# Twelve corner products of a split-fp32 encoder kernel as plain fp32 products of unsplit weights and tokens

## The chip, the cores and the metric

The kernel runs on one core of a Trainium2 chip. The metric is the time of one execution on the device in microseconds (us), lower is better. Engines are named as in the profile: PE is TensorE, DVE VectorE, ACT ScalarE, POOL GpSimd, SP SyncE, whose queue issues nearly all DMAs.

## The reference

A bidirectional encoder layer over 1280 tokens (1024 of a prompt, 256 of a sample), width 1024, all in fp32. What matters here is its beginning: a normalization, a modulation and one wide input projection.

```python
mod = c @ w_ada + b_ada
shift, scale, gate = jnp.split(mod[:, None, :], 3, axis=-1)
h = rms_norm(x, norm_g) * (1.0 + scale) + shift
p = h @ w_in                     # 1024 x 11280 weights
...
g_conv, g_mlstm = jnp.split(jax.nn.sigmoid(gmerge), 2, axis=-1)
merged = g_conv * (y_conv @ w_proj_conv) + g_mlstm * (y_m @ w_proj_mlstm)
return x + gate * (merged @ w_out)
```

The last 2048 columns of `w_in` (from `CGM` on) are the merge gates `gmerge`; the kernel multiplies with these first.

## The kernel before

**Split products.** PE multiplies fp32 operands in a form of one pass (`F32R`) that keeps only a part of the mantissa. To keep precision, each operand is split into a high part (a cast to `F32R`) and a low part (the operand less its high part), and a product is three passes: high x high, high weights x low tokens, low weights x high tokens (`go`, L737 to L760; the matmuls are all on L755). A weight block of 512 x 128 is split by `split_op`: the cast on ACT (L329), the difference on POOL (L330), into one of four `wh` and four `wl` buffers. Tokens are split by `both_parts`: ACT (L383), DVE (L384).

**Strassen.** The projection runs in the form of Strassen's algorithm on 2 x 2 blocks: the contraction of 1024 rows is cut into two halves of four tiles of 128 (k_ = 0 to 3), the tokens into halves of 640, and two column blocks of 128 form a pair. The transposed, modulated tokens are four quarters `B11, B21, B12, B22` of four tiles `xt` each (128 x 640). A pair needs seven products of one weight combination and one token combination each (`Strassen.jobs`), in the order 11 (tokens `b11`), 12 (`b21`), t2, t3, t1, t4, b22. A product is four pieces, one for each k_; a piece is 2 x 3 matmuls of 128 x 320. The weight combinations are made on DVE (`comb`, L628); c1, the first of them, needs both 512 KB halves (`raw`, j = 0 and 1) of the pair's weights. Results are added to earlier ones by DVE (`plus`, L672), which also frees the product's accumulator, one of three in PSUM.

**The corner products.** The products 11 and 12 of the first six pairs (columns 0 to 11 of the merge gates) need no combination. They run first, while the tokens are still being normalized: twelve products, on `b11` or `b21`, of the class `Corner` (L719). For each pair, `corner_load` (L338) fetches both weight blocks as one `raw` tile of 512 KB, and `corner_split` splits one block. There are three `raw` buffers.

**The beginning** (`beginning`, L393 on). SP loads w_ada and the tokens into tiles that later hold token parts; PE multiplies c with w_ada (L480, plain fp32); `norm_x` makes the row sums and scales the tokens (ACT L418, DVE L414 and the small operations L421 to L436); `turn_x` transposes 128 x 128 pieces on PE (L449), three and two at a time into one of two `misc` buffers of PSUM, from where ACT (L454) or DVE (L457) modulate them into `xt`. Groups of token chunks go in the order 0 to 2, 3 to 4, 5 to 7, 8 to 9. `combine` (L389) makes the sums and differences of quarters for t2, t3, t1 and t4, in place.

**What sets the order.** Every operation is recorded with an engine, an assumed duration and a step (`board.step`); `Board.order` then plays the record into one fixed order for each engine, by steps and assumed times. The engines wait for each other's semaphores and run their own lists strictly in order. SP's list is such a list too: a load that waits for its buffer holds up what stands behind it.

Of the kernel before, what the change touches and what calls it, by code (L numbers as in the profile page):

```python
# [9 lines left out]
F32 = mybir.dt.float32  # L10
F32R = mybir.dt.float32r
AF = mybir.ActivationFunctionType
ALU = mybir.AluOpType
# [3 lines left out]
P = 128  # L17
D = 1024
KT = D // P
# [11 lines left out]
TQ = T // 4  # L31
# [150 lines left out]
def encoder_kernel(  # L182
# [134 lines left out]
    def load(kb, dst, src, r, w, low=False):  # L317
        op("SP", kb, lambda: dma(dst(), src), r=r, w=w, low=low)
# [4 lines left out]
    def raw_tile():  # L323
        return buf(wp, [P, 4, 2 * P], F32, "raw", 3)
# [8 lines left out]
    raw_a, early = {}, {}  # L333

    def corner_split(n, j):
        raw = raw_a[n]
        return split_op(lambda: raw[:].rearrange("p a (b c) -> p (a b) c", b=2)[:, 4 * j:4 * j + 4, :], [raw])

    def corner_load(n):

        raw_a[n] = raw = raw_tile()
        load(512, lambda: raw[:].rearrange("p a (b c) -> p (a b) c", b=2), win[:, :, CGM + n * P:CGM + (n + 1) * P], (), [raw])
# [49 lines left out]
    def beginning():  # L392
# [67 lines left out]


# [7 lines left out]
        corner_load(0)  # L469
# [4 lines left out]
        corner_load(2)  # L474
# [10 lines left out]
        corner_load(4)  # L485
# [30 lines left out]
        early.update({(n, j): corner_split(n, j) for j in range(2) for n in (0, 2)})  # L516
        for kt in lows:
            board.step = kt - 6
            for cs in GROUPS[:2]:
                turn_x(cs, [kt])  # L520
            both_parts("b11", B11, [kt])
        for kt in lows:
            board.step = kt // 2 - 2
            for cs in GROUPS[:2]:
                turn_x(cs, [kt + 4])
            both_parts("b21", B21, [kt])
        for k in range(12):
            if k in (0, 2, 4):
                corner_load(6 + k)
            if k == 2:  # L530
                board.step = 0
                for cs in GROUPS[2:]:
                    norm_x(cs)
                for kt in lows:
                    board.step = 0 + kt // 2
                    for cs in GROUPS[2:]:
                        turn_x(cs, [kt, kt + 4])

                board.step = 3
                both_parts("b22", B22)  # L540
                combine(B22, B22, B12)
                board.step = 10
                combine(B12, B12, B11)
                board.step = 4
                combine(B11, B22, B11, ALU.add)
                both_parts("t2", B11)
                board.step = 5
                both_parts("t3", B22)
                board.step = 12
                combine(B21, B21, B11)  # L550
                singles("t1")
                both_parts("t1", B12)
                singles("t4")
                both_parts("t4", B21)
            go(k)
# [163 lines left out]
    class Corner:  # L719


        def __init__(self, n, st):
            self.n, self.st = n, st
            self.jobs = [(None, "b11", self.first), (None, "b21", st.e_12)]

        def first(self, acc):
            self.st.e_11(acc)

        def prep(self, j):
            return early.get((self.n, j)) or corner_split(self.n, j)  # L730

# [5 lines left out]
    def prep(k):  # L737
        if k < len(todo) and k not in made:
            board.step = k - (6 if k < 16 else 2)
            made[k] = todo[k][0].prep(todo[k][1])  # L740
# [466 lines left out]
    corners = {n: Corner(n, sts[n]) for n in sts}  # L1207
    for n, j in ((0, 0), (2, 0), (0, 1), (2, 1), (4, 0), (4, 1), (6, 0), (6, 1), (8, 0), (8, 1), (10, 0), (10, 1)):
        add(corners[n], [j])
# [636 lines left out]
```

## Time and profile before

| | us |
|---|---|
| median of 3 runs | 1730.31 |
| lowest, highest of them | 1727.86, 1730.43 |
| the profiled execution | 1726.71 |
| its span in the trace | 1724.6 |
| PE busy | 1676.9 (97%) |
| DVE, POOL, ACT busy | 974.6, 679.5, 604.4 |
| mean granted clock of PE | 0.992 |

Times within the trace are from the start of the span. PE's matmuls overlap: the duration of one holds its run-out, so what a row of them costs is read from start to start. "x2" is a row of two such instructions, and its duration goes from the first start to the last end. A bracket at the end of a row is the idle time before it and what ended it.

### The profile page before, as it was taken

The page shows a single profiled execution, that of the slowest core. Times are in us where ns is not written, and L with a number is a line of the kernel's source. Part 1 is how long each engine was busy: PE and PEld are TensorE (multiplying, and loading weights), DVE is VectorE, ACT ScalarE, POOL GpSimd, SP SyncE. Part 2 cuts the span into 40 slices and gives each one's busy share as a digit, 9 for nine tenths or more (in the row PEclk, how much of TensorE's full clock was granted, in tenths as well). Part 3 has the DMA queues.
Part 4 walks back from the last instruction along what each step waited for, and adds up shares of the span by engine and source line. Part 5 has one row for each costly group of instructions (what it writes and reads, how often), then busy time and mean ns, then how long its engine had stood idle before and what let it go on. Part 6 is the DMA issues. An engine that isn't in the chain of part 4 may idle for free.

```text
span 1724.6 us, 27940 instructions
## 1 busy us (share of the span) xinstructions
PE 1676.9 (97%) x10702; PEld 1591.3 (92%) x10702; DVE 974.6 (57%) x1657; ACT 604.4 (35%) x1185; POOL 679.5 (39%) x499
## 2 busy tenths in 40 slices
PE   7889999999999999999999999999999999999997
PEld 1789999899999999999999899999888889998986
DVE  1795433456555565566666765642247777565645
ACT  2753333224554222222222222222256565333322
POOL 1124333235665566667766533333210101323412
PEclk9899999999999999999999999999999999999999
DMA  9234323224553222222222434336878865684631
GB/s 332 87 109 146 115 91 121 64 74 122 148 155 108 57 68 68 80 80 63 65 61 89 141 108 138 117 117 231 284 232 273 269 199 162 219 282 135 229 112 61
DMA packets 217562, 241.88 MB, mean 140 GB/s; under 512 B 12645, under 2 KB 174677, under 8 KB 217429
## 3 DMA queue, kind: packets, MB, share of 16 engines
q1 hardware_dynamic: 217248, 240.06, 43.5%
q8 instruction: 85, 1.39, 0.3%
q14 instruction: 49, 0.39, 0.1%
q10 hardware_dynamic: 180, 0.04, 0.0%
HBM read 171.16 MB, written 68.89 MB: 139 GB/s over the span
## 4 chain that ended last, share of the span: by engine, by line
PE 91%; DVE 5%; issue 2%; ACT 1%; DMA 1%; ACTq 0%; SPq 0%; POOL 0%; DVEq 0%; POOLq 0%
PE acc L755 59%; PE u L1365 3%; PE qc L1347 3%; PE accd L1520 2%; PE accd L1521 2%; PE accd L1522 2%; PE accd L1733 2%; PE accd L1734 2%; PE accd L1732 2%; PE acc L1587 2%; PE acc L1588 2%; PE acc L1589 2%; PE acc L480 2%; PE misc L885 1%; PE misc L1408 1%
## 5 line engine op out<-in xcount | busy, mean ns | idle before, releaser
L672 DVE TENSOR_TENSOR q<-acc,q 128x640 f32<-128x640 f32 x272 | 220.6, 820 | 259.9 <-PE acc L755 249.5
L330 POOL TENSOR_TENSOR wl<-comb,wh 128x512 fp32r<-128x512 f32 x176 | 247.2, 1405 | 304.2 <-ACT wh L329 293.2
L330 POOL TENSOR_TENSOR wl<-raw,wh 128x512 fp32r<-128x512 f32 x136 | 191.6, 1409 | 250.9 <-ACT wh L329 245.1
L755 PE MATMUL acc<-xt,wh 128*128 128x320 f32 x1408 | 264.4, 310 | 0.0
L755 PEld LDWEIGHTS acc<-xt,wh 128*128 128x128 f32 x1408 | 220.6, 188 | 0.1
L329 ACT CAST wh<-comb 128x512 fp32r<-128x512 f32 x176 | 108.9, 619 | 243.6 <-PE acc L755 236.1
L329 ACT CAST wh<-raw 128x512 fp32r<-128x512 f32 x136 | 84.4, 621 | 286.5 <-PE acc L755 203.3
L755 PE MATMUL acc<-xt,wl 128*128 128x320 f32 x704 | 160.4, 309 | 0.0
L1548 POOL TENSOR_TENSOR wl<-raw,wh 128x512 fp32r<-128x512 f32 x28 | 36.3, 1300 | 233.7 <-ACT wh L1547 233.7
L755 PEld LDWEIGHTS acc<-xt,wl 128*128 128x128 f32 x704 | 117.7, 188 | 0.0
L628 DVE TENSOR_TENSOR comb<-raw 128x512 f32<-128x512 f32 x88 | 76.7, 872 | 46.7 <-DMA raw<-in_w_in_dram 31.2
L822 POOL TENSOR_TENSOR big<-big,q 128x640 f32<-128x640 f32 x48 | 78.8, 1641 | 37.1 <-DVE q L672 28.8
L572 ACT ACTIVATE q<-q,zero 128x640 f32<-128x640 f32 x76 | 63.2, 831 | 80.4 <-DVE q L672 74.8
L628 DVE TENSOR_TENSOR comb<-raw,comb 128x512 f32<-128x512 f32 x44 | 44.2, 1004 | 78.5 <-POOL wl L330 78.5
L755 PE MATMUL acc<-b00H,wh 128*128 128x320 f32 x352 | 83.0, 316 | 0.0
L755 PE MATMUL acc<-t2L,wh 128*128 128x320 f32 x352 | 80.3, 310 | 2.1 <-DVE t2L L384 2.1
L755 PE MATMUL acc<-b11H,wh 128*128 128x320 f32 x352 | 80.9, 310 | 1.5 <-ACT wh L329 1.5
L755 PE MATMUL acc<-t3H,wh 128*128 128x320 f32 x352 | 81.6, 313 | 0.0
L1520 PE MATMUL accd<-y,wh 128*128 128x320 f32 x256 | 79.9, 313 | 1.5 <-DVE og L1498 1.5
L755 PE MATMUL acc<-t2H,wh 128*128 128x320 f32 x352 | 80.8, 311 | 0.4 <-ACT t2H L383 0.4
L755 PE MATMUL acc<-b10H,wh 128*128 128x320 f32 x352 | 80.6, 309 | 0.4 <-DVE q L672 0.4
L755 PE MATMUL acc<-b11H,wl 128*128 128x320 f32 x352 | 80.1, 308 | 0.9 <-POOL wl L330 0.9
(320 smaller groups left out, 4195.4 us busy)
## 6 DMA issues: line engine op xcount, KB each, us to landing
raw<-in_w_in_dram SPq DMA_DIRECT2D x96, 256.0 KB
raw<-in_w_in_dram SPq DMA_DIRECT2D x46, 512.0 KB
th<-th_dr SPq DMA_DIRECT2D x32, 320.0 KB
th_dr<-q SPq DMA_DIRECT2D x28, 320.0 KB
raw<-in_w_proj_conv_dram SPq DMA_DIRECT2D x16, 512.0 KB
k<-kn_dr SPq DMA_DIRECT2D x64, 128.0 KB
raw<-in_w_proj_mlstm_dram SPq DMA_DIRECT2D x16, 512.0 KB
raw<-in_w_out_dram SPq DMA_DIRECT2D x16, 512.0 KB
```

Source lines behind the costliest of these rows:

```text
L329: op("ACT", .63, lambda: A.copy(wh[:], src()), r=r, w=[wh])
L330: op("POOL", 1.4, lambda: G.tensor_tensor(out=wl[:], in0=src(), in1=fp(wh[:]), op=ALU.subtract), r=[*r, wh], w=[wl])
L480: op("PE", .88, lambda h=h, j=j, kt=kt, wa=wa: PE.matmul(pada[h][0:4, j, :], cz4()[:, kt, :], wa()[:, j * 512:(j + 1) * 512], start=kt == ...
L572: A.activation(out, in_, AF.Tanh, bias=zero[:, 0:1], scale=0.5)
L628: op("DVE", .9, lambda: V.tensor_tensor(out=t[:], in0=x(), in1=y(), op=o), r=[x.tok, y.tok], w=[t])
L672: op("DVE", .82, lambda: V.tensor_tensor(out=two(dst()), in0=acc[:, :, 0:TQ], in1=two(t()), op=ALU.add), r=[acc, t.tok], w=[dst.tok])
L755: PE.matmul(acc[:, q, 0:TQ], st_[:, k_, :], m_[:, q * TQ:(q + 1) * TQ], start=k_ == 0 and n == 0, stop=k_ == 3 and n == 2)
L822: op("POOL", 1.65, lambda: G.tensor_tensor(out=dst(), in0=dst(), in1=t(), op=ALU.mult), r=[dst.tok, t.tok], w=[dst.tok])
L1347: PE.matmul(pq[:, 0:HD + 2], qTs[i][:, kd, c * P:(c + 1) * P], C[:, kd, :], start=kd == 0, stop=kd == 1)
L1365: PE.matmul(pu[:, db, 0:HD + 2], k[:, db * P:(db + 1) * P], wv[:], start=True, stop=True)
L1520: PE.matmul(accs[q][:, :TQ], wh, yH, start=kt == 0, stop=False)
L1548: op("POOL", 1.36, lambda wh=wh, wl=wl, src=src: G.tensor_tensor(out=wl[:], in0=src(), in1=fp(wh[:]), op=ALU.subtract), r=[raw, wh], w=[wl])
```

## The change

The twelve corner products become plain fp32 products: PE reads the unsplit weights in `raw` and the unsplit tokens in `xt`, two matmuls of 128 x 320 for each k_ instead of six. With that `Corner`, `corner_split` and their twelve splits on ACT and POOL go. The order of the twelve changes from pair by pair to first all six on `B11`, then all six on `B21`. A `raw` tile now holds one half (j) of the columns of two pairs, fetched by two DMAs of 256 KB. `b11` and `b21`, the split parts of the first two quarters, are still made, for the later pairs, but recorded beside the combinations. The steps of the preparations of the next products (`prep`) move from k - 6 to k - 8, up to k = 20.

```diff
-    def corner_split(n, j):
-        raw = raw_a[n]
-        return split_op(lambda: raw[:].rearrange("p a (b c) -> p (a b) c", b=2)[:, 4 * j:4 * j + 4, :], [raw])
-
-    def corner_load(n):
-
-        raw_a[n] = raw = raw_tile()
-        load(512, lambda: raw[:].rearrange("p a (b c) -> p (a b) c", b=2), win[:, :, CGM + n * P:CGM + (n + 1) * P], (), [raw])
+    def early_load(j, n):
+
+        raw_a[j, n] = raw_a[j, n + 2] = raw = raw_tile()
+        for i in range(2):
+            c = CGM + (n + 2 * i) * P
+            load(256, lambda i=i: raw[:, :, i * P:(i + 1) * P], win[:, 4 * j:4 * j + 4, c:c + P], (), [(raw, i)])
...
+        def early_product(k, j, x):
+
+            n = 2 * (k % 6)
+            raw, i = raw_a[j, n], n // 2 % 2
+            board.step = k
+            acc = buf(psX, [P, 2, 512], F32, "acc", 3)
+
+            def mm(k_):
+                for q in range(2):
+                    PE.matmul(acc[:, q, 0:TQ], raw[:, k_, i * P:(i + 1) * P], x[k_][:, q * TQ:(q + 1) * TQ],
+                              start=k_ == 0, stop=k_ == 3)
+
+            for k_ in range(4):
+                op("PE", 1.1, lambda k_=k_: mm(k_), r=[(raw, i), (x[k_], 0), (x[k_], 1)] + ([acc] if k_ else []), w=[acc])
+            (sts[n].e_12 if j else sts[n].e_11)(acc)
...
-        early.update({(n, j): corner_split(n, j) for j in range(2) for n in (0, 2)})
-        for kt in lows:
-            board.step = kt - 6
+        for kt in range(KT):
+            board.step = kt - 6 if kt < 4 else kt // 2 - 4
             for cs in GROUPS[:2]:
                 turn_x(cs, [kt])
-            both_parts("b11", B11, [kt])
+        for k in range(6):
+            early_product(k, 0, B11)
...
+        board.step = 1
+        both_parts("b22", B22)
+        combine(B22, B22, B12)
+        board.step = 8
+        both_parts("b11", B11)
+        combine(B12, B12, B11)
+        board.step = 3
+        combine(B11, B22, B11, ALU.add)
+        both_parts("t2", B11)
+        board.step = 4
+        both_parts("t3", B22)
+        for n in (0, 4, 8):
+            board.step = 2 + n // 2
+            early_load(1, n)
+        for k in range(6, 12):
+            early_product(k, 1, B21)
+        board.step = 10
+        both_parts("b21", B21)
+        combine(B21, B21, B11)
...
-            board.step = k - (6 if k < 16 else 2)
+            board.step = k - (8 if k < 20 else 2)
...
-    corners = {n: Corner(n, sts[n]) for n in sts}
-    for n, j in ((0, 0), (2, 0), (0, 1), (2, 1), (4, 0), (4, 1), (6, 0), (6, 1), (8, 0), (8, 1), (10, 0), (10, 1)):
-        add(corners[n], [j])
+    todo.extend([None] * 12)
```

PE's list at the first corner product, before (L449 are transposes; `b00H`, `b00L` are the parts of `B11`):

```order
L449 MATMUL misc<-ident,t3H 128x128 x2
L449 MATMUL misc<-ident,t3L 128x128 x2
L449 MATMUL misc<-ident,b11H 128x128
L449 MATMUL misc<-ident,t3H 128x128 x2
L449 MATMUL misc<-ident,t3L 128x128 x2
L449 MATMUL misc<-ident,b11H 128x128
L449 MATMUL misc<-ident,t3H 128x128 x2
L449 MATMUL misc<-ident,t3L 128x128 x2
L449 MATMUL misc<-ident,b11H 128x128
L755 MATMUL acc<-b00H,wh 128x320 x2
L755 MATMUL acc<-b00L,wh 128x320 x2
L755 MATMUL acc<-b00H,wl 128x320 x2
```

and after (L447 are the transposes, L468 the plain products):

```order
L447 MATMUL misc<-ident,t3H 128x128 x2
L447 MATMUL misc<-ident,t3L 128x128 x2
L447 MATMUL misc<-ident,b11H 128x128
L447 MATMUL misc<-ident,t3H 128x128 x2
L447 MATMUL misc<-ident,t3L 128x128 x2
L447 MATMUL misc<-ident,b11H 128x128
L468 MATMUL acc<-xt,raw 128x320 x2
L447 MATMUL misc<-ident,t3H 128x128 x2
L447 MATMUL misc<-ident,t3L 128x128 x2
L447 MATMUL misc<-ident,b11H 128x128
L468 MATMUL acc<-xt,raw 128x320 x2
```

The first piece of a product stands behind ten transposes instead of fifteen, and one piece follows each group of transposes; 34 pieces follow the last.

DVE's list where the corner products end, before: the last low parts (t1, t4), the sums, then the combinations for the first pair's last product and the second pair.

```order
L384 TENSOR_TENSOR xt_1062<-xt_152,xt_1024 128x640
L384 TENSOR_TENSOR xt_1071<-xt_153,xt_1035 128x640
L384 TENSOR_TENSOR xt_1079<-xt_154,xt_1045 128x640
L672 TENSOR_TENSOR q_1087<-acc_980,big_468 128x640
L672 TENSOR_TENSOR q_1095<-acc_1026,q_1087 128x640
L672 TENSOR_TENSOR big_468<-acc_1026,big_468 128x640
L628 TENSOR_TENSOR comb_1099<-raw_745,comb_814 128x512
L672 TENSOR_TENSOR q_1087<-acc_1064,q_1087 128x640
L628 TENSOR_TENSOR comb_1107<-raw_823,raw_857 128x512
L628 TENSOR_TENSOR comb_1112<-comb_1107,raw_823 128x512
```

and after (`q_771` is the sum of the last corner product, `raw_716` and `raw_736` are the second pair's weights, L382 the low parts of t4, `big_396<-acc_729` the sum of t2):

```order
L683 TENSOR_TENSOR q_771<-acc_697,q_594 128x640
L639 TENSOR_TENSOR comb_784<-raw_716,raw_736 128x512
L639 TENSOR_TENSOR comb_803<-comb_784,raw_716 128x512
L382 TENSOR_TENSOR xt_812<-xt_151,xt_748 128x640
L639 TENSOR_TENSOR comb_821<-raw_716 128x512
L382 TENSOR_TENSOR xt_831<-xt_152,xt_758 128x640
L382 TENSOR_TENSOR xt_843<-xt_153,xt_769 128x640
L382 TENSOR_TENSOR xt_851<-xt_154,xt_786 128x640
L683 TENSOR_TENSOR big_396<-acc_729,big_396 128x640
```

The second pair's combinations now stand ahead of the low parts of t4 and of the sum of t2.

POOL's list from its first split on, after (before, twelve splits of `raw` tiles of the corner products stand ahead of those of the combinations; `comb_695`, `comb_700`, `comb_704`, `comb_710` are the first pair's combinations, `raw_643` and `raw_685` its weights, and the second pair's `raw_736` goes into the buffer of `raw_685`):

```order
L330 TENSOR_TENSOR wl_712<-comb_700,wh_706 128x512
L330 TENSOR_TENSOR wl_726<-comb_704,wh_714 128x512
L330 TENSOR_TENSOR wl_746<-comb_695,wh_720 128x512
L330 TENSOR_TENSOR wl_761<-raw_685,wh_724 128x512
L330 TENSOR_TENSOR wl_794<-comb_710,wh_780 128x512
```

The split that reads `raw_685` is the fourth in the row.

## Rows read from the trace of the kernel before

**Rows 1.** The page, part 4: shares of the chain that ended last, by engine.

```profile
PE 91%; DVE 5%; issue 2%; ACT 1%; DMA 1%; ACTq 0%; SPq 0%; POOL 0%; DVEq 0%; POOLq 0%
```

**Rows 2.** Table by stretches: length; busy us of PE, PEld, DVE, ACT, POOL; clock; DMA.

```profile
140.00:160.00 20.00, 20.00 (x139) 20.00 (x138) 10.35 (x13) 6.23 (x9) 6.67 (x7) 1.00 0.37 113
```

**Rows 3.** Timeline of PE, 43 to 70 us: start, duration, line, operation, count, wait.

```profile
43.55 0.33 PE L449 MATMUL misc<-ident,t3H 128*128 128x128 f32 x1 [3.60 <-DVE t3H L436]
...
50.60 0.69 PE L449 MATMUL misc<-ident,t3H 128*128 128x128 f32 x2
...
51.70 0.88 PE L755 MATMUL acc<-b00H,wh 128*128 128x320 f32 x2
...
54.85 0.46 PE L755 MATMUL acc<-b00H,wl 128*128 128x320 f32 x2
...
69.29 0.27 PE L449 MATMUL misc<-ident,t2L 128*128 128x128 f32 x1
...
69.39 0.27 PE L449 MATMUL misc<-ident,t2H 128*128 128x128 f32 x1
```

**Rows 4.** Timeline of PE, 84 to 88 us: first matmuls of two products.

```profile
84.11 0.45 PE L755 MATMUL acc<-b00H,wh 128*128 128x320 f32 x2
...
87.62 0.45 PE L755 MATMUL acc<-b10H,wh 128*128 128x320 f32 x2
```

**Rows 5.** Timeline of PE, 105 to 133 us: products t2 to b22 of the first pair.

```profile
106.01 0.46 PE L755 MATMUL acc<-t2H,wh 128*128 128x320 f32 x2
...
110.97 0.56 PE L755 MATMUL acc<-t2L,wh 128*128 128x320 f32 x2 [2.10 <-DVE t2L L384]
...
113.09 0.73 PE L755 MATMUL acc<-t2L,wh 128*128 128x320 f32 x2
...
117.59 0.75 PE L755 MATMUL acc<-xt,wh 128*128 128x320 f32 x4
...
126.28 0.57 PE L755 MATMUL acc<-b11H,wh 128*128 128x320 f32 x2 [1.49 <-ACT wh L329]
...
131.05 0.47 PE L755 MATMUL acc<-t2H,wh 128*128 128x320 f32 x2
```

**Rows 6.** Timeline of PE: plain fp32 matmuls of L1347 and L480.

```profile
1296.04 1.03 PE L1347 MATMUL qc<-C,qT 128*128 128x258 f32 x4
...
1296.91 1.03 PE L1365 MATMUL u<-wv,k 128*128 128x258 f32 x4
...
14.68 3.60 PE L480 MATMUL acc<-b00L,big 128*4 128x512 f32 x8
...
18.11 3.60 PE L480 MATMUL acc<-b10H,big 128*4 128x512 f32 x8
```

**Rows 7.** Timeline of POOL and DVE, 38 to 43 us.

```profile
38.37 3.73 POOL L330 TENSOR_TENSOR wl<-raw,wh 128x512 fp32r<-128x512 f32 x3 [14.09 <-ACT wh L329]
...
40.21 0.67 DVE L504 SCALAR_TENSOR_TENSOR s<-big,cols 128x16 f32<-128x16 f32 x1
...
41.08 1.03 DVE L428 TENSOR_TENSOR rt<-rr 128x3 f32<-128x3 f32 x1
...
42.15 0.16 DVE L429 TENSOR_TENSOR rt<-rt,ssq 128x3 f32<-128x3 f32 x1
```

**Rows 8.** Timelines of SP's queue and DVE: a load and its first reader.

```profile
129.14 0.39 SPq L318 DMA_DIRECT2D raw<-in_w_in_dram  x1
...
133.12 0.81 DVE L628 TENSOR_TENSOR comb<-raw 128x512 f32<-128x512 f32 x1 [1.04 <-DMA raw<-in_w_in_dram]
```

**Rows 9.** Timelines of POOL and DVE, 112 to 134 us.

```profile
129.29 4.09 POOL L330 TENSOR_TENSOR wl<-comb,wh 128x512 fp32r<-128x512 f32 x3 [1.33 <-ACT wh L329]
...
115.24 3.02 DVE L384 TENSOR_TENSOR xt<-xt 128x640 fp32r<-128x640 f32 x4
...
126.93 1.57 DVE L628 TENSOR_TENSOR comb<-comb,raw 128x512 f32<-128x512 f32 x1
...
131.25 0.82 DVE L672 TENSOR_TENSOR big<-acc,big 128x640 f32<-128x640 f32 x1 [1.54 <-PE acc L755]
```

More of the change, by code (lines that the diff above doesn't have):

```diff
@@ L331, in split_op @@
         return wh, wl
-    raw_a, early = {}, {}
-    def corner_split(n, j):
-        raw = raw_a[n]
-        return split_op(lambda: raw[:].rearrange("p a (b c) -> p (a b) c", b=2)[:, 4 * j:4 * j + 4, :], [raw])
-    def corner_load(n):
-        raw_a[n] = raw = raw_tile()
-        load(512, lambda: raw[:].rearrange("p a (b c) -> p (a b) c", b=2), win[:, :, CGM + n * P:CGM + (n + 1) * P], (), [raw])
+    raw_a = {}
+    def early_load(j, n):
[3 more added lines that the diff above has]
+            load(256, lambda i=i: raw[:, :, i * P:(i + 1) * P], win[:, 4 * j:4 * j + 4, c:c + P], (), [(raw, i)])
     xt = {jl: [buf(xp, [P, TH2], F32, "xt", 17, xp.tile([P, TH2], F32, tag="xt", name="xt")) for _ in range(4)]
@@ L468, in beginning @@
             load_wa(kt)
-        corner_load(0)
+        early_load(0, 0)
         for kt in range(5, KT):
@@ L473, in beginning @@
             load_x(c)
-        corner_load(2)
+        early_load(0, 4)
         pada = [buf(psX, [P, 2, 512], F32, "acc", 3) for _ in range(2)]
@@ L484, in beginning @@
             load_x(c)
-        corner_load(4)
+        early_load(0, 8)
         mods = {}
@@ L515, in beginning @@
             norm_x(cs)
-        early.update({(n, j): corner_split(n, j) for j in range(2) for n in (0, 2)})
-        for kt in lows:
-            board.step = kt - 6
+        for kt in range(KT):
+            board.step = kt - 6 if kt < 4 else kt // 2 - 4
             for cs in GROUPS[:2]:
                 turn_x(cs, [kt])
-            both_parts("b11", B11, [kt])
-        for kt in lows:
[L523 to L555, printed above, removed]
+        for k in range(6):
+            early_product(k, 0, B11)
@@ new lines, in beginning @@
+        board.step = -1
+        for cs in GROUPS[2:]:
+            norm_x(cs)
+        for kt in lows:
+            board.step = -1 + kt // 2
+            for cs in GROUPS[2:]:
+                turn_x(cs, [kt, kt + 4])
+        board.step = 1
[8 more added lines that the diff above has]
+        board.step = 4
@@ L556, in beginning @@
+        both_parts("t3", B22)
[7 more added lines that the diff above has]
+        combine(B21, B21, B11)
+        singles("t1")
+        both_parts("t1", B12)
+        singles("t4")
+        both_parts("t4", B21)
         at[0] = 12
@@ L717, in corner_place @@
         return corner_places[i]
[L719 to L730, printed above, removed]
     todo, made, at = [], {}, [0]
```

## The prediction, made before the change was run

> **What bounds the kernel now.** The page's chain of waits comes first: TensorE (PE) makes 91% of the chain that ends last [rows 1], so a change is worth what it takes from or adds to PE's line, and other engines count where PE waits for them. The table by stretches comes second: from 140 us on PE is busy for all of 20 us at full clock [rows 2]. PE's order is the same in both programs from the first pair of gate columns on, and that of the other engines from the third pair on, so what the change does must show by one mark: the start of the second pair's first product, at 131.05 us in the trace of before [rows 5]. The rest is a shift.
>
> The timeline of PE up to that mark comes third. The first transpose of the tokens stands at 43.55 [rows 3]. From there to 131.05 are 87.5 us. What PE has to do in them at full clock: a split product takes 3.51 us (84.11 to 87.62) [rows 4], so twelve corner products are 42.1 and five of the first pair 17.6; 80 transposes at 0.107 (69.29 to 69.39) [rows 3] are 8.6. That is 68.3, so 19.2 us are lost. I place them so. The first product stands at 51.70, behind fifteen transposes, while DVE normalizes: 6.5 lost. The clock then is at the lower level, 1.2 GHz, until about 54.5, some 2.8 us behind the first product (by 54.85 two matmuls take 0.46 instead of 0.73 us) [rows 3, 5]: 1.4. Products t2 and t3 should take 7.0 but last from 106.01 to 117.59: 4.55 lost, 2.10 of them a wait for the low part of t2 from DVE and about 1.8 a second spell at 1.2 GHz behind it (0.73 us for two matmuls) [rows 5]. The first pair's last product waits for its weights (1.49 and more at 126.28): 117.59 to 131.05 is 13.46 for 10.5, 2.9 lost [rows 5]. The remaining 3.8 are short waits between transposes at 65 to 95 us.
>
> **The change, part by part.**
>
> 1. PE's work. A split product issues 24 matmuls of 320 columns at 0.1463 us each. A plain fp32 one issues 8, and each is two instructions in the trace: L1347 has two for each 258 columns, and four start to start take 0.87 us (1296.04 to 1296.91), 0.2175 each; L480 has eight of 512 columns in 3.43 us (14.68 to 18.11), 0.429 each [rows 6]. Scaled to 320 columns these two bounds give 0.270 and 0.268; I take 0.269. So one product is 16 x 0.269 = 4.31 us, twelve 51.7: **9.6 us more work**. The weight loads stay hidden: L1347 loads 128 x 128 fp32 at the 0.2175 pace, shorter than 0.269. The Trainium skill (FP8 and Floating Point Precision, TensorE Precision Notes) says a true fp32 product takes four passes; taken as four against three passes of the split form, that would make 56.2 and 14.1 more. The rows decide against that ratio, as a 320-column pass of the split form already costs 0.146 where a quarter of the plain one costs 0.1345.
>
> 2. The start. POOL's early weight splits go: its first split is now one of the first pair. In before three of them run from 38.37 for 3.73 us, and in that stretch tiny DVE operations take 0.67 and 1.03 us instead of 0.16 [rows 7]. These stand on the way to the first transpose. The Trainium skill (SBUF — State Buffer, SBUF: two separate sides) says that DVE and GpSimd share a pair of ports under a lock held for a whole instruction; the 1.03 agrees with it. Of the excess 0.51 + 0.87 I take **1.2 us**. The order of PE's instructions further puts the first product behind ten transposes instead of fifteen, without a cast before it: the eleventh starts at 50.60 [rows 3], and a product in its place would stand at about 50.7. So the first product moves from 51.70 to 50.7 - 1.2 = **49.5**, with 70 transposes left instead of 65.
>
> 3. The corner on PE. If nothing waits, product 10 of 12 ends at 49.5 + 1.4 (the same spell at low clock) + 70 x 0.107 + 40 x 1.077 = **101.5**, and product 12 at 110.1. The short waits between transposes I cost at nothing: each group of transposes now has a 1.08 us piece of plain product, ready since its weights need no split, in front of the next, and evacuating it takes DVE and ACT no longer than that. If this cover fails, up to 3.8 us return. The parts b00 and b10 are now made behind the transposes; when the transposes are through, at 49.5 + 1.4 + 7.5 + 14 pieces x 1.077 = 73.5, DVE has some 28 operations of 0.755 to make (3.02 for four) [rows 9], 21 us, and so the parts of t2 and t3 are ready before PE asks for them at 110. The 4.55 go. The weight combinations of all products of the first pair now stand in one row on DVE, ahead of the low parts of t4, so the 2.9 for the last product go too.
>
> 4. The new wait. Raw weight tiles are now read by PE itself, so each of the three buffers is held until its two products end, where before ACT and POOL emptied it ahead of them. The second half of the first pair (raw_685) can be fetched only when product 10 ends, 101.5. A 512 KB load lands about 3.9 us after its issue (129.14 to 133.12, where DVE waits for it) [rows 8]. Then: two combinations on DVE 1.4, cast 0.7, and on POOL four splits in a row of 1.36 (4.09 for three) [rows 9] = 5.45, of which the fourth reads raw_685. Only then SP can load raw_736 into that buffer: 3.9. DVE meanwhile stands at comb_784, which needs raw_736, with everything behind it: combinations 2.05, four low parts of t4 3.0, and the sum that frees the accumulator of t2, 0.82 [rows 9]. Product t4 needs both the low part and that accumulator. Sum 101.5 + 3.9 + 1.4 + 0.7 + 5.45 + 3.9 + 5.9 = 122.75. Where POOL and DVE meet, a combination took 1.57 where another took 0.81 [rows 8, 9]; I add 0.4: **123.1**. PE asks for t4 at 110.1 + 3 x 3.51 = 120.6, so it **waits 2.5 us**. Bounds: with no collision and loads of 3.4 us 1.1; with two collisions and loads of 4.4 4.5.
>
> 5. The clock behind that wait. In before a wait of 2.10 with shorter ones around it was followed by a spell at 1.2 GHz (1.8 us), the one of 1.49 with another just behind it was not [rows 5]. I take half, 0.9; ends 0 and 1.8.
>
> Sum: t4 123.1 + 2 x 3.51 + 0.9 = **131.0** at the mark, against 131.05: **no change**. The profiled execution took 1726.7 us for its span of 1724.6, which is 3.6 under the median of the runs shown, 1730.3; a change of 0.0 on that median is 1730.3. A measurement can tell about 0.2%, 3.5 us, from no change.
>
> **The rivals.**
>
> A, the gain stays. The loads land in 3.4 us, nothing collides, and the clock rises as early against the denser start as the better of the two cases allows: 1.4 less from the wait, 0.9 from the clock behind it, up to 1.4 from the first spell, at most 3.7 in all: 1726.6. For it: t2 and b22 waits worth 7.4 us go for certain. Against it: the chain of part 4 hangs on product 10, so an earlier PE only waits longer unless the loads are short. Chance 0.17 for more than 3.5 us.
>
> B, slower by the wait for t4. Its place is DVE at comb_784, its price whatever DVE ends behind 120.6. At 4.5 us of wait and a following spell of 1.8 the mark is 133.9, and with the lost cover of one more microsecond among the transposes 134.9: 1734.2. It decides from the point where raw_736 lands later than about 119, 2.2 us later than in my sum, or POOL's splits take 1.7 instead of 1.36 in a row. For it: 1.57 for one combination [rows 9]. Against: POOL has nothing else then. Chance 0.14.
>
> C, plain products cost more than their two passes say. On the Trainium skill's four against three passes (part 1) they would cost 4.5 us more than in my sum. As a mechanism of this kernel: at 0.293 per instruction, twice the split form's 0.146, forty pieces before product 10 end 3.8 us later, and all behind them: 134.8, 1734.1. Against it stands that L1347 runs at 0.2175 for 258 columns [rows 6]. Chance 0.06.
>
> **How the numbers follow.** Forecast, within 0.2%: 0.63; A 0.17; B and C 0.20. The forecast alone spans 1727.0 to 1733.6. The range of 1726.5 to 1734.5 takes in A and the nearer part of B and C, and leaves out some 2 in 10.
>
> **What would show it.** The 192 plain instructions some 0.27 us apart; the first one at 49 to 50 us; no DVE operation of a few columns over 0.3 us before 43; product t2 without a wait at 110; a PE wait of 1 to 4.5 us ahead of t4, named by DVE, with DVE idle for about 5 us before a combination that waits for a DMA; the second pair at 129 to 134. I am wrong if PE waits among the transposes again, if t2 waits, or if t4 doesn't.

## The result, and the profile after

The changed kernel takes 1733.19 us (median of 8 runs, 1731.75 to 1733.95), the kernel before, on the same chip, 1727.93 (8 runs, 1725.92 to 1730.43). The ratio is 1.0028, 95% interval 1.0017 to 1.0039: slower by about 5 us. The forecast was no change, 1730.3. Its range of 1726.5 to 1734.5 holds the time, but the slowdown is clear of the noise and none was forecast.

| | before | after |
|---|---|---|
| profiled execution, its span (us) | 1726.71, 1724.6 | 1732.88, 1731.1 |
| PE busy | 1676.9 | 1684.3 |
| POOL, ACT busy | 679.5, 604.4 | 662.7, 598.7 |
| first transpose, first corner product | 43.55, 51.70 | 41.94, 48.88 |
| product t2 of the first pair | 106.01 | 109.13 |
| second pair's first product, the mark | 131.05 | 136.68 |

The mark is 5.6 us later, the span 6.5, so nearly all of it happened ahead of the mark. PE's share of the chain that ended last has fallen from 91% [rows 1]. Page of the changed kernel, part 4:

```profile
PE 88%; DVE 3%; issue 1%; ACT 1%; DMA 0%; SPq 0%; DVEq 0%; ACTq 0%
```

The table by stretches of the changed kernel (columns as in [rows 2]) shows where:

```profile
80.00:100.00 20.00, 20.00 (x76) 14.13 (x75) 16.67 (x22) 10.61 (x15) 0.00 (x0) 1.00 0.40 134
100.00:120.00 20.00, 20.00 (x108) 17.07 (x106) 12.59 (x13) 8.09 (x12) 8.76 (x5) 1.00 0.44 135
120.00:140.00 20.00, 13.05 (x72) 12.99 (x72) 15.47 (x17) 4.98 (x7) 6.05 (x4) 0.74 0.36 117
140.00:160.00 20.00, 20.00 (x139) 20.00 (x138) 9.24 (x11) 6.23 (x9) 7.79 (x6) 1.00 0.44 135
```

From 80 us on PE has no gap up to 120 us, and then loses 6.95 of 20 us and a quarter of its clock. The timeline of PE, changed kernel, names the place (L447 transposes, L468 plain products, L753 split products):

```profile
41.94 0.33 PE L447 MATMUL misc<-ident,t3H 128*128 128x128 f32 x1 [2.23 <-DVE t3H L434]
...
48.88 2.16 PE L468 MATMUL acc<-xt,raw 128*128 128x320 f32 x4
...
51.42 1.24 PE L468 MATMUL acc<-xt,raw 128*128 128x320 f32 x4
...
72.76 36.77 PE L468 MATMUL acc<-xt,raw 128*128 128x320 f32 x136
...
109.13 0.69 PE L753 MATMUL acc<-t2H,wh 128*128 128x320 f32 x2
...
127.04 1.41 PE L753 MATMUL acc<-xt,wh 128*128 128x320 f32 x4 [6.95 <-DVE big L683]
...
128.77 1.27 PE L753 MATMUL acc<-xt,wh 128*128 128x320 f32 x4
...
130.37 1.27 PE L753 MATMUL acc<-xt,wh 128*128 128x320 f32 x4
...
133.16 0.46 PE L753 MATMUL acc<-b11H,wh 128*128 128x320 f32 x2
...
136.68 0.46 PE L753 MATMUL acc<-t2H,wh 128*128 128x320 f32 x2
```

Product t4 starts 6.95 us late, for the sum that frees t2's accumulator (L683 on DVE). Behind the wait its pieces stand 1.6 us apart (128.77 to 130.37) instead of 0.88, and the table by stretches gives a granted clock (the third number from the end) of 0.50 there, the lower level of 1.2 GHz:

```profile
129.00:131.00 2.00, 2.00 (x9) 2.00 (x9) 1.67 (x3) 0.60 (x1) 0.00 (x0) 0.50 0.28 106
```

So t4 lasts 6.1 us (127.04 to 133.16) where 3.5 are needed. That is 6.95 + 2.6 = 9.55 us lost at one place. Without them the mark would stand at 127.1, 3.9 ahead of its place in before.

The chain that leads there, from the timelines of SP's queue, DVE and POOL (L639 combinations, L387 the four subtractions of the token combination for t4, L382 low parts of t4, L330 splits):

```profile
100.95 0.38 SPq L318 DMA_DIRECT2D raw<-in_w_in_dram  x1
...
107.27 7.64 SPq L318 DMA_DIRECT2D raw<-in_w_in_dram  x2
...
105.22 0.69 DVE L639 TENSOR_TENSOR comb<-raw 128x512 f32<-128x512 f32 x1 [3.43 <-DMA raw<-in_w_in_dram]
...
108.49 6.69 DVE L387 TENSOR_TENSOR xt<-xt 128x640 f32<-128x640 f32 x4
...
118.79 0.69 DVE L639 TENSOR_TENSOR comb<-raw 128x512 f32<-128x512 f32 x1 [2.88 <-DMA raw<-in_w_in_dram]
...
121.54 4.62 DVE L382 TENSOR_TENSOR xt<-xt 128x640 fp32r<-128x640 f32 x3
126.07 0.82 DVE L683 TENSOR_TENSOR big<-acc,big 128x640 f32<-128x640 f32 x1
...
107.37 5.29 POOL L330 TENSOR_TENSOR wl<-comb,wh 128x512 fp32r<-128x512 f32 x3 [105.16 <-ACT wh L329]
112.62 1.88 POOL L330 TENSOR_TENSOR wl<-raw,wh 128x512 fp32r<-128x512 f32 x1
...
121.09 3.46 POOL L330 TENSOR_TENSOR wl<-comb,wh 128x512 fp32r<-128x512 f32 x2 [4.75 <-ACT wh L329]
```

Read it as a sum. PE lets go of the buffer and the load is issued at 100.95; 4.27 to DVE's combination at 105.22; 2.15 to POOL's first split at 107.37; 7.13 for four splits, to 114.50; the second load of the SP row is issued then (107.27 + 7.64 less 0.38, or 114.53); 4.26 from there to the second pair's combination at 118.79, before which DVE stands with the low parts of t4 behind it; 8.25 from there to t4 at 127.04.

### The profile page after: what moved, and what is told of

Its sections match the earlier page's. It is cut to its first block, busy times and chain, and to the rows that moved or that the text cites. A ratio compares the mean times of both kernels' runs of the same rounds, so it can differ in the third digit from the quotient of the medians.

```text
span 1731.1 us, 27712 instructions
## 1 busy us (share of the span) xinstructions
PE 1684.3 (97%) x10606; PEld 1585.6 (92%) x10606; DVE 972.3 (56%) x1657; ACT 598.7 (35%) x1173; POOL 662.7 (38%) x487
## 3 DMA queue, kind: packets, MB, share of 16 engines
q8 instruction: 84, 1.38, 0.3%
## 4 chain that ended last, share of the span: by engine, by line
PE 88%; DVE 3%; issue 1%; ACT 1%; DMA 0%; SPq 0%; DVEq 0%; ACTq 0%
PE acc L753 59%; PE u L1361 3%; PE qc L1343 3%; PE accd L1516 2%; PE accd L1517 2%; PE accd L1518 2%; PE accd L1729 2%; PE accd L1730 2%; PE accd L1728 2%; PE acc L1583 2%; PE acc L1584 2%; PE acc L1585 2%; PE misc L883 1%; PE misc L1404 1%; PE misc L1444 1%
## 5 line engine op out<-in xcount | busy, mean ns | idle before, releaser
L330 POOL TENSOR_TENSOR wl<-comb,wh 128x512 fp32r<-128x512 f32 x176 | 248.6, 1413 | 404.0 <-ACT wh L329 395.0
L683 DVE TENSOR_TENSOR q<-acc,q 128x640 f32<-128x640 f32 x272 | 220.6, 820 | 265.5 <-PE acc L753 255.3
L753 PE MATMUL acc<-xt,wh 128*128 128x320 f32 x1408 | 266.7, 312 | 6.9 <-DVE big L683 6.9
L330 POOL TENSOR_TENSOR wl<-raw,wh 128x512 fp32r<-128x512 f32 x124 | 173.9, 1403 | 176.5 <-ACT wh L329 170.3
L753 PEld LDWEIGHTS acc<-xt,wh 128*128 128x128 f32 x1408 | 222.5, 189 | 7.3 <-issue 7.2
L329 ACT CAST wh<-raw 128x512 fp32r<-128x512 f32 x124 | 77.0, 621 | 267.9 <-PE acc L753 207.5
L753 PE MATMUL acc<-xt,wl 128*128 128x320 f32 x704 | 161.5, 311 | 0.0
L1544 POOL TENSOR_TENSOR wl<-raw,wh 128x512 fp32r<-128x512 f32 x28 | 36.2, 1298 | 234.1 <-ACT wh L1543 227.6
L753 PEld LDWEIGHTS acc<-xt,wl 128*128 128x128 f32 x704 | 118.4, 189 | 0.0
L639 DVE TENSOR_TENSOR comb<-raw 128x512 f32<-128x512 f32 x88 | 79.0, 897 | 46.4 <-DMA raw<-in_w_in_dram 22.1
L639 DVE TENSOR_TENSOR comb<-raw,comb 128x512 f32<-128x512 f32 x44 | 45.1, 1024 | 78.5 <-POOL wl L330 78.5
L753 PE MATMUL acc<-t3H,wh 128*128 128x320 f32 x352 | 81.6, 313 | 0.0
L1516 PE MATMUL accd<-y,wh 128*128 128x320 f32 x256 | 80.0, 313 | 1.5 <-DVE og L1494 1.5
L753 PE MATMUL acc<-b11H,wh 128*128 128x320 f32 x352 | 80.8, 310 | 0.0
L753 PE MATMUL acc<-t3L,wh 128*128 128x320 f32 x352 | 80.8, 311 | 0.0
L753 PE MATMUL acc<-t2H,wh 128*128 128x320 f32 x352 | 80.8, 311 | 0.0
L753 PE MATMUL acc<-t3H,wl 128*128 128x320 f32 x352 | 80.6, 311 | 0.0
L753 PE MATMUL acc<-t2H,wl 128*128 128x320 f32 x352 | 80.2, 309 | 0.0
L1517 PE MATMUL accd<-y,wh 128*128 128x320 f32 x256 | 80.2, 313 | 0.0
```

The source lines that it names most:

```text
L329: op("ACT", .63, lambda: A.copy(wh[:], src()), r=r, w=[wh])
L330: op("POOL", 1.4, lambda: G.tensor_tensor(out=wl[:], in0=src(), in1=fp(wh[:]), op=ALU.subtract), r=[*r, wh], w=[wl])
L639: op("DVE", .9, lambda: V.tensor_tensor(out=t[:], in0=x(), in1=y(), op=o), r=[x.tok, y.tok], w=[t])
L683: op("DVE", .82, lambda: V.tensor_tensor(out=two(dst()), in0=acc[:, :, 0:TQ], in1=two(t()), op=ALU.add), r=[acc, t.tok], w=[dst.tok])
L753: PE.matmul(acc[:, q, 0:TQ], st_[:, k_, :], m_[:, q * TQ:(q + 1) * TQ], start=k_ == 0 and n == 0, stop=k_ == 3 and n == 2)
L1516: PE.matmul(accs[q][:, :TQ], wh, yH, start=kt == 0, stop=False)
```

## The experiments

Theory: the wait is an order on DVE (the second pair's combination ahead of t4's low parts and t2's sum) that becomes a wait because a load is late, and the load is late because PE holds raw buffers and because DVE and POOL lengthen each other. Main rival: the 9 us of extra matmul time are simply the loss. Every ratio is to the kernel before on the same chip.

**1. The order on DVE.** One number is changed, so that the preparations of products 17 to 19 get later steps; the low parts of t4 and the sum then stand ahead of the second pair's combination.

```diff
-            board.step = k - (8 if k < 20 else 2)
+            board.step = k - (8 if k < 17 else 2)
```

> Theory (the wait for t4 is a place in DVE's list, behind combinations that wait for a load): with the four low parts of t4 and the sum that frees the accumulator of t2 standing ahead of the second pair's first combination, they run from about 116 on and end by 119 to 121, so t4 starts at 120 to 121.5 instead of 127.0, the spell at the lower clock behind it goes, and the second pair's first product stands at 127.5 to 130 instead of 136.7: about 1725 us, 7 to 9 less than the change as made. Rival (the 9.4 us of added matmul time are the loss, and the wait only sits where it shows): a wait of the same size comes back at the next product whose weights are late, the second pair's first one, and the time stays at 1731 to 1734.

Measured: 1723.88 us, ratio 0.9973 (0.9962 to 0.9984). PE has no wait between 100 and 160 us. PE's and DVE's timelines in this run, first piece of t4, then the mark, then the low parts and the combination behind them:

```profile
121.74 0.75 PE L753 MATMUL acc<-xt,wh 128*128 128x320 f32 x4
...
128.78 0.46 PE L753 MATMUL acc<-t2H,wh 128*128 128x320 f32 x2
...
118.66 3.60 DVE L382 TENSOR_TENSOR xt<-xt 128x640 fp32r<-128x640 f32 x4
122.18 0.82 DVE L683 TENSOR_TENSOR q<-acc,big 128x640 f32<-128x640 f32 x1
122.91 0.68 DVE L639 TENSOR_TENSOR comb<-raw 128x512 f32<-128x512 f32 x1
```

With the same matmuls and later loads (this run's second load is issued at 116.6) the wait and the slow spell are gone. The main rival falls: the added matmul time did not make the loss. This version also beats the kernel before.

**2. The steps of before.** The same order undone in another way, by the change's own last hunk.

```diff
-            board.step = k - (8 if k < 20 else 2)
+            board.step = k - (6 if k < 16 else 2)
```

> The change with one of its parts undone: the steps of the preparations go back to k - 6 up to k = 16. In this order DVE has the low parts of t4 and the sum of t2 ahead of the second pair's first combination. Theory (DVE's order makes the wait): no wait for t4 of over 1 us, no spell at the lower clock behind it, second pair's first product at 128 to 131, about 1724 to 1726, as in the run where only the late limit of the steps was moved. Rival (the wait comes from the raw buffers alone and this part of the change has no share in it): 1732 to 1734.

Measured: 1725.80, ratio 0.9986 (0.9977 to 0.9994); wait for t4 1.29, no slow spell, mark at 129.18. PE's timeline:

```profile
122.07 0.82 PE L753 MATMUL acc<-xt,wh 128*128 128x320 f32 x4 [1.29 <-DVE big L683]
```

As the theory said, but for the 1.29 (it said at most 1). So the plain products without the new steps gain a little, about 2 us; with them they lose.

**3. The steps alone, in the kernel before.**

```diff
-            board.step = k - (6 if k < 16 else 2)
+            board.step = k - (8 if k < 20 else 2)
```

> The kernel before with one part of the change alone: the preparations' steps at k - 8 up to k = 19, the corner products still split. Theory (an early combination harms only where its load is late; split products empty the raw buffers ahead of PE): DVE does not stand before a combination by more than 2 us, no wait for t4 over 2 us, 1726 to 1731. Rival (the steps alone make the wait): a wait of 4 to 8 us at the first pair, 1732 to 1737.

Measured: 1729.26, ratio 1.0005 (0.9996 to 1.0013). The time is the theory's. But a wait of the rival's size is there: 4.98 us, at t1, for its low part on DVE, and the mark in the trace is at 133.42, 2.4 later than in before. PE's timeline:

```profile
120.80 0.90 PE L755 MATMUL acc<-xt,wh 128*128 128x320 f32 x2 [4.98 <-DVE xt L384]
```

DVE did not stand before a load there, it was only full. The times can't tell these 2.4 us from none: their interval reaches to 1.0013, 2.2 us, and the stretch from the mark to the end, where PE has the same work in both, took 1593.55 us in the profiled execution of before and 1591.68 in this one. The steps alone do not cost what the change costs.

**4. One raw buffer free a tile earlier.** The last early tile is loaded into a `wl` and a `comb` buffer, both idle then.

```diff
+        if (j, n) == (1, 8):
+            raw_a[1, 8] = a = buf(wp, [P, 4, P], F32R, "wl", 4)
+            raw_a[1, 10] = b = buf(cp, [P, 4, P], F32, "comb", 5)
...
```

> The last early weight tile (columns 8 to 11, second half) lies in two buffers that are idle at that time, so one raw buffer is free a tile earlier; PE's list is unchanged. Theory (the wait begins with buffers that PE holds): the first pair's halves are fetched at about 74 and 92 us instead of 92 and 101, so the combinations, splits and the next load come some 8 us earlier, t4 waits less than 0.5 us, no spell at the lower clock follows, and the second pair's first product stands at 127 to 128.5: about 1724.5 us, 8 to 9 less than the change as made. Rival (the reload hangs on POOL's splits and their collisions, not on PE's hold): less than 3 us gained, about 1731.

Measured: 1725.68, ratio 0.9984 (0.9975 to 0.9992). The first combination stands at 97.09 instead of 105.22, t4 does not wait, and the mark is at 129.16 (expected 127 to 128.5). A wait of 0.92 is left at t1, for the sum of the last corner product: it stands at 118.53, three products of 3.51 ahead of the mark. PE's hold on the buffers is shown as the other half of the cause. The timelines of DVE, POOL and PE in this run hold a second reading: with POOL idle between 107.7 and 114.6, the same four subtractions (here L394) take 3.02 us, not 6.69.

```profile
109.60 3.02 DVE L394 TENSOR_TENSOR xt<-xt 128x640 f32<-128x640 f32 x4
...
106.41 1.26 POOL L330 TENSOR_TENSOR wl<-raw,wh 128x512 fp32r<-128x512 f32 x1 [2.98 <-PE acc L476]
114.59 1.46 POOL L330 TENSOR_TENSOR wl<-comb,wh 128x512 fp32r<-128x512 f32 x1 [6.92 <-ACT wh L329]
...
118.53 0.82 PE L761 MATMUL acc<-xt,wh 128*128 128x320 f32 x4 [0.92 <-DVE q L691]
```

**5. Both mends together** (1 and 4).

> The late limit of the steps moved and the last early tile in idle buffers, together. Theory (both act on one wait, which is gone with the first alone): no further gain worth a microsecond, 1723 to 1724.5, no wait for t4; the 0.9 us that were left with the tile alone go. Rival (each takes away a wait of its own): gains add, 1716 to 1719.

Measured: 1724.94, ratio 0.9984 (0.9975 to 0.9992); no wait for t4, and none at t1. (The 0.9 us of which the expectation speaks stood at t1.) The gains do not add: it was one wait.

**6. What the collision on POOL's side costs.** The four subtractions for t4 are cut from 640 columns to 16; everything else keeps its place.

```diff
...
-        combine(B21, B21, B11)
+        combine(B21, B21, B11, c=16)
```

> The change as made, with the four subtractions that make the token combination of t4 cut from 640 columns to 16: the other 624 columns of that combination are left out; the order of all engines stays. DVE is then free while POOL makes the first pair's four splits. Theory (the two lengthen each other): the four splits take 5.2 to 5.5 instead of 7.1 us, the load behind them is issued 1.6 to 1.9 us earlier, t4 starts 1.6 to 1.9 earlier against product t2, and the wait is 5.0 to 5.4 instead of 6.95. Rival (1.76 is what a split costs there with or without DVE): 7.1 and 6.9 again.

Measured: 1730.25, ratio 1.0006 (0.9995 to 1.0018). POOL's and PE's timelines:

```profile
108.72 4.19 POOL L330 TENSOR_TENSOR wl<-comb,wh 128x512 fp32r<-128x512 f32 x3 [106.51 <-ACT wh L329]
112.86 1.31 POOL L330 TENSOR_TENSOR wl<-raw,wh 128x512 fp32r<-128x512 f32 x1
...
126.63 1.41 PE L753 MATMUL acc<-xt,wh 128*128 128x320 f32 x4 [5.21 <-DVE big L683]
```

Four splits take 5.45 us (108.72 to 114.17) instead of 7.13, and the wait is 5.21 instead of 6.95: 1.7 us of it were DVE's subtractions in POOL's way, as the theory had it.

**7. The start.** Three early splits, read by nobody, are put back. The first try split tiles that land early, so only one split was left when DVE worked on its small operations, and that one fell into its pause before a result of PE:

```diff
+        for n in (0, 0, 4):
+            split_op(lambda n=n: raw_a[0, n][:, :, 0:P], [(raw_a[0, n], 0)])
```

> Three casts on ACT and three differences on POOL of the first weight tiles come back at the start; nothing reads them. Theory (the start was won because POOL no longer works beside DVE's small operations): these operations take 0.5 to 1.0 us each again where POOL works, the first transpose stands at 43.0 to 43.6 instead of 41.94, the first product at about 50.2 instead of 48.9, and all behind it, the chain of the wait too, moves by the same: about 1734.5. Rival (the start was won by PE's order alone): first transpose and time as in the change as made, 41.9 and 1733.

Measured: 1734.13, ratio 1.0030 (1.0017 to 1.0043), first transpose at 42.34, not 43.0 to 43.6. As a test it missed its place. The second try takes all three from the tile that lands last (`for n in (4, 4, 4)`).

> As the run with three early splits, but all three on the second raw tile, which lands later, so that POOL works between about 38 and 42 us beside DVE's small operations. Theory (POOL beside them makes them long): at least two operations of a few columns take 0.5 to 1.1 us instead of 0.16, and from DVE's first modulation operation to its first scaling of tokens (1.38 us in the change as made, 2.75 in before) it takes 2.2 to 2.8 again; product and chain behind it move by the same, about 1734.5. Rival (the length of these operations has another cause): 1.4 us, 1733.

Measured: 1734.47, ratio 1.0042 (1.0027 to 1.0058). POOL's, DVE's and PE's timelines of that run:

```profile
38.55 3.72 POOL L330 TENSOR_TENSOR wl<-raw,wh 128x512 fp32r<-128x512 f32 x3 [36.32 <-ACT wh L329]
...
40.39 0.68 DVE L518 SCALAR_TENSOR_TENSOR s<-big,cols 128x16 f32<-128x16 f32 x1
41.00 1.30 DVE L520 COPY shf<-big 128x16 f32<-128x16 f32 x1
...
44.02 0.48 PE L447 MATMUL misc<-ident,t3H 128*128 128x128 f32 x1 [3.89 <-DVE t3H L434]
```

From DVE's first modulation operation (40.17) to its first scaling of tokens (43.21) it takes 3.0 us; in the change as made 1.38, in before 2.75. That part of the gain at the start is POOL's absence, and worth about 1.4 us in the trace; the times alone do not show it, as the interval of this run overlaps that of the change as made (1.0017 to 1.0039). What else the first product gains, 2.82 us in all, was not taken apart; PE's order, with ten transposes ahead of it instead of fifteen, is the candidate. (First transposes of kernels without early splits lie between 41.1 and 43.1, so a single difference of that size in two traces proves little; the stretch between the two operations does.)

**8. Half plain.** The second six products go back to split form; their weights are split while the first six run.

```diff
...
+        board.step = 2
+        both_parts("b21", B21)
         for k in range(6, 12):
-            early_product(k, 1, B21)
+            split_product(k)
         board.step = 10
-        both_parts("b21", B21)
```

The parts of `b21`, which these products read, are made at step 2 instead of 10; `split_product` is the three passes of the split form.

> The first six products stay plain; the second six go back to split products, whose weights ACT and POOL split while the first six run. Theory: six products at 3.51 instead of 4.28 give 4.6 us, and since the splits empty the raw buffers early, the first two pairs' loads come early and t4 does not wait: the second pair's first product at 122.5 to 125, about 1720 us. Rival (POOL's six splits beside DVE's modulations and low parts hold up transposes or parts between 60 and 85 us): up to 4 of that is lost again, 1724. Second rival (added matmul time is the loss, the wait is not): 1728 to 1729.

Measured: 1733.00, ratio 1.0026 (1.0017 to 1.0035), a miss: 4.6 us less matmul time and no gain, with a wait of 8.96 us. It is not at t4 but at t1, for the accumulator of the last corner product: it ends at 123.33, and t1, t4 and b22 (10.5 us, and 2.7 for the lower clock) lie between that and the mark at 136.55. DVE stood 5.45 us before the first pair's combination, whose load was late, since POOL needed 11.9 us for two splits. PE's, DVE's and POOL's timelines:

```profile
123.33 1.40 PE L777 MATMUL acc<-xt,wh 128*128 128x320 f32 x4 [8.96 <-DVE q L707]
...
94.91 0.69 DVE L663 TENSOR_TENSOR comb<-raw 128x512 f32<-128x512 f32 x1 [5.45 <-DMA raw<-in_w_in_dram]
...
73.76 11.88 POOL L330 TENSOR_TENSOR wl<-raw,wh 128x512 fp32r<-128x512 f32 x2 [4.82 <-ACT wh L329]
```

The same with the steps of before (as in experiment 2):

> The half plain form with the steps of before (k - 6 up to 16). With the steps of the change that form waited 9.0 us for t4, behind DVE, which had itself stood 5.5 us before a combination that waits for a load; that load came late because two POOL splits took 11.9 us beside DVE's additions and low parts at 74 to 86 us. Theory (POOL beside a DVE without gaps is the price of split products here): those splits are as long as before, and moving combinations back by some steps regains only part: t4 still waits 4 to 8 us, 1727 to 1732. Rival (the order of DVE alone): no wait at t4, 1720 to 1722.

Measured: 1723.93, ratio 0.9974 (0.9965 to 0.9982): here the rival was right about the wait, which is gone at t1 as at t4 (the expectation places it at t4), and the splits are as slow as before; the time lies between the two forecasts. What is left is another wait of the same kind, 2.60 us for the accumulator of an earlier product, whose sum stands on DVE behind the late combination. POOL's, DVE's and PE's timelines of that run:

```profile
74.89 10.04 POOL L330 TENSOR_TENSOR wl<-raw,wh 128x512 fp32r<-128x512 f32 x1 [4.79 <-ACT wh L329]
...
77.09 3.03 DVE L387 TENSOR_TENSOR xt<-xt 128x640 f32<-128x640 f32 x4
80.04 3.02 DVE L382 TENSOR_TENSOR t3L<-xt,t3H 128x640 fp32r<-128x640 f32 x4
...
96.36 0.69 DVE L663 TENSOR_TENSOR comb<-raw 128x512 f32<-128x512 f32 x1 [5.78 <-DMA raw<-in_w_in_dram]
...
105.02 0.87 PE L490 MATMUL acc<-b10H,wh 128*128 128x320 f32 x2 [2.60 <-DVE q L707]
```

and its table by stretches just behind that wait (the granted clock is 0.50, and stays there until 111.2, so for 6.2 us and not the 4 of the next expectation):

```profile
106.00:108.00 2.00, 2.00 (x9) 2.00 (x9) 2.00 (x3) 1.38 (x3) 0.91 (x2) 0.50 0.43 164
```

So the preparations were moved later still, to `k - (4 if k < 16 else 2)`, with the combinations behind the sums:

> The half plain form with the preparations at k - 4 up to k = 15, so that DVE has the low parts of t2 and the sums of three products ahead of the first pair's combinations. In the run with k - 6 DVE stood 5.8 us before a combination whose load was late, with the sum of the eighth product behind it, and PE waited 2.6 us for that accumulator, followed by 4 us at the lower clock. Theory (one list in order is the cause each time): the 2.6 and the spell behind it go, no new wait over 1 us, second pair's first product at 124 to 126.5, 1719 to 1721.5. Rival (DVE has too much to do by then, in any order): t2 or t4 waits instead, by 2 to 6 us, 1723 to 1727.

Measured: 1719.48, ratio 0.9952 (0.9937 to 0.9966), the mark at 122.48 (below the expected 124 to 126.5), t4 waits 0.30. PE's timeline at the mark:

```profile
122.48 0.46 PE L777 MATMUL acc<-t2H,wh 128*128 128x320 f32 x2
```

It beats both kernels, the one before by about 8 us.

**9. What a plain product costs when nothing waits.** The same late steps with all twelve products plain, and with none.

> The change as made with the preparations at k - 4 up to k = 15, all twelve products plain. Theory (order makes the wait; each plain product costs 0.77 us more than a split one, and that cost comes through in full once nothing waits): no wait for t4 over 1 us, 4.6 us more than the half plain form with the same steps (1719.5 beside 1727.9 of before): about 1724. Rival (the plain products' time is hidden by something else, or the half plain form won by its earlier loads): within 1.5 us of the half plain form, or over 1728.

Measured: 1724.13, ratio 0.9982 (0.9973 to 0.9991), no wait for t4, mark at 127.31:

```profile
127.31 0.46 PE L753 MATMUL acc<-t2H,wh 128*128 128x320 f32 x2
```

Six more plain products than in the half plain form cost 4.8 us at the mark (127.31 - 122.48) and 0.0030 of 1728, 5.2 us, in the ratios; six times 0.77 are 4.6. The longer matmul time comes through in full.

> All twelve products split again, but in the new order (six on the first quarter, then six on the second) and with the preparations at k - 4 up to k = 15. Theory: 4.6 us less matmul time than the half plain form; but POOL's early splits work beside DVE's small operations again and the low parts of the first quarter stand before the first product, so the first product moves from about 49 back to 51 to 52, and parts and weights of the first six must keep pace: 1717 to 1722. Rival (the low parts and splits of the first six hold PE up between 50 and 75 us by more than the 4.6 they save): 1722 to 1727, with waits among the first six products.

Measured: 1726.90, ratio 0.9998 (0.9989 to 1.0007): the rival's time, but not by the rival's waits. The first product stands at 52.68, 0.7 later than the theory said, no split product among the first six waits, and then PE waits 6.29 us ahead of t1, for the accumulator of the last corner product. PE's and DVE's timelines:

```profile
117.77 1.41 PE L779 MATMUL acc<-xt,wh 128*128 128x320 f32 x4 [6.29 <-DVE q L709]
...
103.52 6.71 DVE L387 TENSOR_TENSOR xt<-xt 128x640 f32<-128x640 f32 x4
110.16 6.74 DVE L382 TENSOR_TENSOR xt<-xt 128x640 fp32r<-128x640 f32 x8
```

The sum that PE waits for (116.81) is behind four subtractions and eight low parts on DVE: an engine that is full, not one that waits for a load. So in this order the first six plain products earn their longer time, by taking splits and low parts from the start, and the second six do not. That it must be so in any order is not shown. With t1 right behind t3, which ends at 111.3, and at full clock the mark of this run would stand at about 121.9 (an estimate: 111.3 and three products of 3.51), level with the 122.48 of the half plain form. An order in which DVE gets to that sum in time was not tried for the form with all products split.

## Why the prediction was wrong

**The sum of PE's work (part 1) was right.** The last 34 pieces take 36.37 us (72.76 to 109.13), 0.2674 per instruction, against 0.269. Rival C, with its price of four against three, falls: at 0.293 these pieces would take 39.8. That is the price alone; how many passes PE makes, no run shows.

**The start (part 2) was right in the main.** The first product stands at 48.88, predicted 49.5. Of the excess in DVE's small operations 1.37 went, predicted 1.2.

**The corner without waits (part 3) was right.** No wait among the transposes behind the first product, t2 at 109.13 (110.1), no wait at t2 or b22. With no wait at t4 the prediction's own numbers give 120.6 + 7.0 = 127.6 at the mark; experiment 9 shows 127.31, and 1724.1 us.

**The wait for t4 (part 4) stood where it was said, for the reason that was said, at nearly three times its size, and this is the step that failed.** Link by link, predicted and measured: release of the buffer 101.5, 100.95; loads 3.9, 4.27 and 4.26; combination and cast 2.1, 2.15; four splits 5.45, 7.13; DVE from the late combination to t2's sum freed 5.9, 8.25. The term that was mis-sized is "Where POOL and DVE meet ... I add 0.4": 1.7 on POOL's side (experiment 6) and 2.35 behind the second load, where two splits of 1.73 meet low parts of 1.54 (4.62 for three, where [rows 9] has 3.02 for four). The first was taken away in a run, the second is read from the trace alone. So 4.0 instead of 0.4. One meeting was seen in [rows 9] and taken for an exception; that the change puts four subtractions beside four splits, and low parts beside the next two, stood in the orders of both engines and was not multiplied out. The upper bound of the wait, 4.5, with "two collisions", had the same fault.

**The clock behind the wait (part 5)**: 0.9 taken, 2.6 measured, above its upper end of 1.8. Its two ends came from what followed waits of 1.49 and 2.10 us; behind this one the granted clock stayed at 0.50 for 5.6 us (127.04 to 132.6).

Together: 3.9 later at t4 and 1.7 more behind it, from 131.0 to 136.68, outside the 129 to 134 given for the mark. That the time still lies in the range is luck. The range reached 4.2 us above the 1730.3 on which it was built; the kernel before took 1727.93 beside the changed one, and the difference between the two is 5.3. Rival B is what happened: its place, and its second point of decision (splits at 1.7 in a row; 1.78 measured). It had 0.14 of the chances, because "POOL has nothing else then" was held against it. That is true of POOL and says nothing of DVE. The idle time of DVE ahead of the late combination, given as about 5 us, was 2.88: the lengthened subtractions had filled much of the rest (with them cut, in experiment 6, it was 5.92).

The Trainium skill (SBUF — State Buffer, SBUF: two separate sides) says that a DVE operation with two inputs in SBUF and a GpSimd operation that reads SBUF exclude each other for a whole instruction, and that the later one is blocked. Experiments 4 and 6 agree: by that rule subtraction and split should take turns, and in the trace of after one pair of them follows the next every 1.83 us (subtractions start at 109.59, 111.42 and 113.26), where alone they take 0.755 and 1.30. That is 0.2 less than the two together, so not the whole of both durations excludes the other.

## What to carry to other kernels

When a change frees a buffer later, follow the engine that stands, in order, behind the reload, and ask whether something that is already there could stand ahead of the operation that waits; here one number in an order was worth 9 us, more than the whole change. Where two engines are known to lengthen each other, price every meeting that the two orders show side by side, at the pair's measured rate, and not one as a surcharge. And a change that adds work on the bounding engine can still win by what it takes from others, but only where those others hold the bounding engine up: in the orders tried, six plain products did, the next six did not.

## What the runs showed that was not expected

- A POOL split of 128 x 512 that takes 1.3 us alone took 10.04 us (74.89 to 84.93 in experiment 8) while DVE ran low parts and subtractions without a gap; DVE lost nothing meanwhile (3.03 and 3.02 for four, 0.755 each). In the changed kernel at 108 us the two took turns instead, at 1.9 us each. What decides between the two patterns was not tried.
- Under POOL's splits even operations of 16 columns wait: 1.30 us for a copy of 128 x 16 that takes 0.17 without (experiment 7).
- The granted clock stayed at 1.00 (2.4 GHz) behind waits of 0.92, 1.29 and 2.01 us (experiments 4, 2, 8). It was 0.50 (1.2 GHz) for 6.2 us behind one of 2.60 (experiment 8), for 4.5 behind one of 6.29 (experiment 9), for 5.6 behind the 6.95 of the change and for 5.8 behind one of 8.96 (experiment 8). In before, behind a wait of 2.10, it was 0.50 from 112.5 to 115.9 [rows 5]. So two waits as close as 2.01 and 2.10 us differ in what followed, and the longest spell stands behind one of the shorter waits: the length of the wait alone does not give the length of the spell.
- The end of such a chain is worth more than its wait: 6.95 us of wait cost 9.55.
